# Moving tiles of four feed-forward layers, begun at four different byte offsets

## The chip, the core and the metric

The kernel runs on one core of one Trainium2 chip. The time is device microseconds of one execution of the whole program; a profile gives the span from the first to the last instruction of one such execution. One unit returns all through: the **pitch** of matmuls, which is the time from the start of one matmul to the start of the next.

## The reference

The input is 256 rows of 1024 float32 numbers. Nine stages follow one another: `ffn_a0`, `mla`, `ffn_b0`, `ffn_a1`, `nsa`, `ffn_b1`, `final` (a norm with a gain), `mix` and `peer`. The four stages named `ffn` are the feed-forward layers in question, and each of them computes

```
h = h + 0.5 * swiglu(rmsnorm(h, g), w_gate, w_up, w_down)
swiglu(x) = (silu(x @ w_gate) * (x @ w_up)) @ w_down     # 1024 -> 2816 -> 1024
```

The stages between them are attention mixers (`mla`, `nsa`, `mix`), and `peer` multiplies the rows with two tables of 16384 x 1024 numbers and combines them by gates.

## The kernel before

Every matrix product is made of three. Each float32 operand is split into a high part in the type that TensorE multiplies in one pass (`fp32r`) and the rest, the low part; high by high, high by low and low by high are summed in PSUM. `Stream` reads all weights in the order of use, in pieces of 128x1024, by SyncE's DMAs. ScalarE makes the high part (`wh`, lines 180 and 189) and VectorE the low part (`wl`, lines 204 and 209). Each half of a piece is multiplied by the norm's gain on the way where there is one.

At the end of each stage `down` adds the product to the 256 rows in `c.x` and makes the operand of the next stage. `Norm` transposes the rows by TensorE (line 331), ScalarE copies them out of PSUM into the tile `xth` (high part, line 338) and VectorE writes the rest into `xtl` (line 339). Each tile has 8 slices of 256 columns, one for each 128 of the 1024 input numbers. The rows' factors `rstd` are made beside that by `rstd_of` (ScalarE line 318, GpSimd lines 320 and 322) and are applied after the product.

In `ffn` the weights are the stationary operand, 128x128 at a time, and a slice of `xth` or `xtl` is the moving operand, 128x256 (lines 581 to 583). A chunk is 256 of the 2816 hidden numbers for gate and up. It takes 8 slices x 4 blocks x 3 products = 96 matmuls. With 11 chunks a layer has 1056 such matmuls, and the four layers have 4224. Each matmul has a weight load of its own, of 128 columns. The mixers use the same tiles the other way round: `xth` and `xtl` are stationary there and the weights move (`linear`, line 261). In `peer` weights are stationary again (line 1645), with 3072 matmuls on a slice of `xth` or `xtl` and 384 on the tiles `gb` and `qbd`.

`Lined` places tiles of 256 bytes and more on multiples of 256 bytes within a partition, `LINE`. Small tiles such as `ss`, `ms`, `rstd` and `nm`, of 32 bytes per buffer, stand behind one another in the same pool. Weight tiles begin on such a multiple, and a block of 128 weights is 512 bytes, so every weight load begins on one. The list `OFF` gives, in elements of 4 bytes, where in `xth` the slices begin, for each `Norm` that `down` makes; the first layer's comes from `take_norm`. Before, `xth` is padded by 48 elements and `xtl` by 16; `xtl` stands right behind `xth`, with no filling, that is 192 bytes past a multiple of 256, and its slices begin at `(off + 16) % 64`. Counted from a multiple of 256 bytes, the high and low slices therefore begin at the same byte: at 192 (48 elements) in the four feed-forward layers and in `peer`, and at 0 in `mla`, `nsa` and `mix`. A slice is 1024 bytes, so all eight slices of a tile have the same offset.

`flush` puts the leftovers of one chunk (its evacuation, and a matmul on line 552 that spreads the row factors) into the next chunk's first matmuls.

Of the kernel before, what the change touches and what calls it, by code (L numbers as in the profile page):

```python
# [8 lines left out]
F32R = mybir.dt.float32r  # L9
# [7 lines left out]
P = 128  # L17
D = 1024
NT = 2
KD = D // P  # L20
# [19 lines left out]
    _n += _w  # L40
NCOLS = _n + 8
LINE = 256
OFF = [0, 48, 48, 0, 48, 0, 48]


class Lined:


    def __init__(self, pool, late=False):
        self.pool, self.tags, self.late, self.over = pool, set(), late, 0  # L50

    def fill(self, name):
        if name == "xtl":
            return
        if self.over:
            self.pool.tile([P, (LINE - self.over) // 4], F32, name=name + "_fill", tag=name + "_fill", bufs=1)
        self.over = 0
# [197 lines left out]
def rounds(nc, sets, start, stop):  # L255

    for p, (a, b) in enumerate(((0, 0), (0, 1), (1, 0))):
        for out, st_, mv in sets:  # L260
            nc.tensor.matmul(out, st_[a], mv[b], start=start and p == 0, stop=stop and p == 2)  # L261
# [9 lines left out]
def ps_tile(c, tag, name):  # L271
    return c.psum.tile([P, 512], F32, name=name, tag="bank", bufs=8)


def uid(c, s):
    c.n += 1
    return f"{s}_{c.n}"


def lined(c, pool):  # L280
    return c.lines.setdefault(pool, Lined(pool, pool is c.pool))


def wt(c, shape, tag, bufs, dt=F32):
    return lined(c, c.pool).tile(shape, dt, name=uid(c, tag), tag=tag, bufs=bufs)


def st(c, shape, tag, bufs, dt=F32):
    return c.sp.tile(shape, dt, name=uid(c, tag), tag=tag, bufs=bufs)
# [23 lines left out]
def rstd_of(c, src, n):  # L313

    nc = c.nc
    junk = c.sp.tile([P, D], mybir.dt.bfloat16, name=uid(c, "junk"), tag="junk", bufs=1)
    ss = wt(c, [P, 1], "ss", 4)
    nc.scalar.activation(junk[:, :n], src, AF.Square, accum_out=ss)
    m = wt(c, [P, 1], "ms", 4)
    nc.gpsimd.tensor_scalar(m, ss, 1.0 / n, EPS, op0=ALU.mult, op1=ALU.add)  # L320
    r = wt(c, [P, 1], "rstd", 8)
    nc.gpsimd.tensor_tensor(r, m, c.mhalf, op=ALU.pow)
    return r

# [50 lines left out]
def behind(t, off):  # L375

    return t[:, off:off + KD * 256].rearrange("p (k q) -> p k q", k=KD)


class Norm:  # L380
# [2 lines left out]

    def __init__(self, c, off=0):
        self.c = c
        self.hi = behind(wt(c, [P, KD * 256 + 48], "xth", 1, F32R), off)
        self.lo = behind(wt(c, [P, KD * 256 + 16], "xtl", 1, F32R), (off + 16) % 64)
        self.rs = [None] * NT

    def turn(self, t, half):  # L390
# [2 lines left out]
    def stats(self, t):  # L393
        self.rs[t] = rstd_of(self.c, self.c.x[t], D)
# [13 lines left out]
class FinalNorm(Norm):  # L408
# [9 lines left out]
    def again(self, t):  # L418
        r_ = rstd_of(self.c, self.c.x[t], D)
        self.c.nc.gpsimd.tensor_tensor(self.rs[t], self.rs[t], r_, op=ALU.mult)  # L420
# [17 lines left out]
def take_norm(c, kind=Norm):  # L438
    n = c.norm
    c.norm = None  # L440
    if n is None:
        n = kind(c, 48)
        n.all()
    return n.hi, n.lo, n.rs

# [35 lines left out]
def down(c, hi, lo, KT, scale, nxt, rate=0):  # L481
# [26 lines left out]
    if nxt:  # L508
        n = c.norm = nxt(c, OFF[c.norms])
        c.norms += 1  # L510
# [22 lines left out]
def ffn(c, nxt):  # L533

    nc = c.nc
    with c.tc.tile_pool(name=uid(c, "ffn"), bufs=1) as pool:
        c.sp = pool = Lined(pool)
        hi, lo, rs = take_norm(c)
        ah = pool.tile([P, NFT, 256], F32R, name=uid(c, "ah"))
        al = pool.tile([P, NFT, 256], F32R, name=uid(c, "al"))  # L540
# [56 lines left out]
class Attn:  # L597
# [40 lines left out]
    def post(self, i, u, ops):  # L638
        c, nc = self.c, self.c.nc
        nh = u[2]  # L640
        s = self.rows() if self.rows else st(c, [P, 512], "s", self.ns)
        nm = wt(c, [P, 4], "nm", 4)
        ps = self.ps.pop(i)
        for h in range(nh):
            sl = slice(h * u[3], (h + 1) * u[3])
            nc.vector.tensor_tensor_reduce(s[:, sl], ps[:, sl], ops.bias(u, h), -ops.scale, -PAD, ALU.add, ALU.min,  # L646
                                           nm[:, h:h + 1])
        if self.sink is not None:
            self.e[i] = self.sink(u, nm)
        self.s[i] = s, nm  # L650
# [90 lines left out]
def mla(c, nxt):  # L741
    nc = c.nc
    scale = (MN + MR) ** -0.5
    with c.tc.tile_pool(name="mla", bufs=1) as pool:
# [5 lines left out]
        if 2:  # L750
            c.ws.segment(c.ends["mla_wo"], pool, 2, 3)
        rope, causal = (c.early[n] for n in ("rope", "causal"))
        hi, lo, rs = take_norm(c)
        cq = [T([P, MQ], f"cq{t}") for t in range(NT)]
        ckv = [T([P, MKV + MR], f"ckv{t}") for t in range(NT)]
# [22 lines left out]
        def evac_in(ci, t, ps):  # L778
            if ci == 0:
                nc.scalar.activation(cq[t], ps, AF.Copy, scale=rs[t])  # L780
                rq[t] = rstd_of(c, cq[t], MQ)
                c.pend.append(lambda: transpose_to(c, cq[t], t, cqh, cql, [0, 1, 2], "mla_q_norm"))
            else:
                nc.scalar.activation(ckv[t], ps, AF.Copy, scale=rs[t])
                rkv[t] = rstd_of(c, ckv[t][:, :MKV], MKV)
                nc.gpsimd.tensor_copy(kr[t], ckv[t][:, None, MKV:])
                rotate(kr[t], t, 1)
                c.pend.append(lambda: transpose_to(c, ckv[t], t, ckh, ckl, [0, 1], "mla_kv_norm"))
# [171 lines left out]
def nsa(c, nxt):  # L960
    nc = c.nc
    with c.tc.tile_pool(name="nsa", bufs=1) as pool:
# [15 lines left out]
        h1 = T([P, 2, GG, 16], "h1")  # L978
        h1r = T([P, GG, 4, 16], "h1r")
        hi, lo, rs = take_norm(c)  # L980
        r8, rneg = [], []

# [639 lines left out]
def peer(c, nxt):  # L1622
# [4 lines left out]
    with ExitStack() as ctx:  # L1627
# [7 lines left out]
        n = Norm(c, 48)  # L1635
# [28 lines left out]
        with c.tc.tile_pool(name="peer1", bufs=1) as pp:  # L1664
# [138 lines left out]
            n = len(work)  # L1803
# [14 lines left out]
        with c.tc.tile_pool(name="peer2", bufs=1) as pp:  # L1818
# [40 lines left out]
            def prep(n):  # L1859

                if n >= NK:
                    return
                i = V_ORDER[n]
                a = stage[i // 4][:, (i % 4) * 256:(i % 4 + 1) * 256]
                nc.vector.tensor_tensor(a, a, G[:, i], op=ALU.mult)
                if n < 2:
                    h, l = (pp.tile([P, 256], F32R, name=uid(c, t), tag=t, bufs=3) for t in ("hj", "hg"))
                else:
                    h, l = ring[0][:, n % 4, 0], ring[0][:, n % 4, 1]
                nc.scalar.activation(h, a, AF.Copy)  # L1870
                nc.vector.tensor_sub(l, a, h.bitcast(F32))  # L1871
                C[n] = h, l
                if n % 4 == 3:
                    del stage[i // 4]
                    load(n // 4 + 2)

            ring = []
            hot(0)
            b = 0
# [11 lines left out]
                    hot(b + 1)  # L1891
                    b += 1

            ring.append(wt(c, [P, 8 * 256 + 16], "xtl", 1, F32R)[:, 16:][:, :2048].rearrange("p (a b q) -> p a b q", a=4, b=2))
            acc = [[ps_tile(c, "acc", uid(c, "acc")) for _ in range(2)] for t in range(NT)]
            for n in range(NK - 2):
                w = [c.ws.next() for _ in range(2)]
                prep(n + 2)
                h, l = C.pop(n)
                a = n == 0  # L1900
                tss = [slice(t * P, (t + 1) * P) for t in range(NT)]
                rounds(nc, [(acc[t][f], (h[:, ts], l[:, ts]), w[f]) for f in range(2) for t, ts in enumerate(tss)],
                       a, False)
                if n == 8:
                    xr = wt(c, [P, NT * D + 48], "xth", 1)[:, :NT * D].rearrange("p (t d) -> p t d", t=NT)
                    for t in range(NT):
                        nc.gpsimd.dma_start(xr[:, t], xs[t])
            w = {(n, f): c.ws.next() for n in (NK - 2, NK - 1) for f in range(2)}
# [166 lines left out]
```

## Time and profile before

| what | value |
|---|---|
| median of 3 runs | 2009.03 us (2008.43 to 2010.54) |
| the profiled execution, whole time | 2011.29 us |
| its span | 2009.5 us |
| granted TensorE clock, mean over the span | 0.994 |
| TensorE matmuls, busy share | 98% |
| VectorE, busy share | 74% |

The whole time of the profiled execution is its span and 1.8 us around it. A busy TensorE is not TensorE at its peak: the record of a 128x256 matmul is 276 ns long, but the next one starts after some 113 ns. How fast TensorE gets on is read from the starts, or from the number of matmuls in a stretch without idle time.

### The profile page before, as it was taken

How to read it: one execution, taken by the hardware profiler on the slowest of the kernel's cores; microseconds unless marked ns; L12 is line 12 of the kernel's file. 1: busy time of each engine (PE TensorE's matmuls, PEld its weight loads, DVE VectorE, ACT ScalarE, POOL GpSimd, SP SyncE). 2: the span in 40 equal slices, each digit the busy share in tenths (PEclk: the TensorE clock that was granted, in tenths of full speed). 3: DMA queues.
4: the chain of work that ended last, by engine and by line, in shares of the span. 5: the costliest groups of instructions: out<-in, count | busy, mean ns of one | idle time of the engine just before them, and what ended most of it. 6: DMA issues, size and time to landing. Idle time of an engine off the chain costs nothing.

```text
span 2009.5 us, 35124 instructions
## 1 busy us (share of the span) xinstructions
PE 1978.0 (98%) x13284; PEld 1806.2 (90%) x13284; DVE 1488.9 (74%) x2747; ACT 1099.9 (55%) x1803; POOL 329.7 (16%) x398
## 2 busy tenths in 40 slices
PE   8999999999999999999999999999999999999999
PEld 8998989988998877899887789999999998888887
DVE  6765667765875788777489878999688877767675
ACT  6554756544554467665387655445444545554543
POOL 2210413202330432332044100000000000000000
PEclk9999999999999989999999999999999999999999
DMA  6665425664766322376643565776654548777774
GB/s 213 196 197 164 144 90 193 195 203 160 248 225 217 125 77 87 124 259 200 199 148 106 166 201 180 251 243 229 212 180 167 168 158 285 239 243 244 236 250 158
DMA packets 105385, 380.76 MB, mean 189 GB/s; under 512 B 12032, under 2 KB 12224, under 8 KB 104960
## 3 DMA queue, kind: packets, MB, share of 16 engines
q1 hardware_dynamic: 93600, 335.76, 51.1%
q0 software_dynamic: 11616, 42.77, 6.3%
q8 instruction: 104, 1.70, 0.4%
q14 instruction: 65, 0.53, 0.1%
HBM read 360.63 MB, written 17.85 MB: 188 GB/s over the span
## 4 chain that ended last, share of the span: by engine, by line
PE 88%; DVE 7%; ACT 2%; issue 2%; POOL 2%; DMA 0%; SPq 0%; ACTq 0%; DVEq 0%; POOLq 0%
PE acc L261 30%; PE A L1645 17%; PE gu L582 8%; PE gu L583 8%; PE gu L581 8%; PE lin L261 5%; PE G L1843 3%; PE acc L268 2%; PE q L1645 2%; DVE wl L209 2%; PE up L261 1%; PE tr L331 1%; DVE wl L204 1%; DVE s L646 1%; PE po L841 1%
## 5 line engine op out<-in xcount | busy, mean ns | idle before, releaser
L180 ACT ACTIVATE wh<-raw 128x1024 fp32r<-128x1024 f32 (+1 forms) x402 | 422.5, 1057 | 333.0 <-issue 142.2
L204 DVE TENSOR_TENSOR wl<-raw,wh 128x1024 fp32r<-128x1024 f32 (+1 forms) x402 | 486.0, 1219 | 130.0 <-PE acc L261 95.0
L209 DVE SCALAR_TENSOR_TENSOR wl<-raw,cols_sb,wh 128x512 fp32r<-128x512 f32 (+4 forms) x488 | 412.7, 896 | 70.2 <-ACT wh L189 35.2
L582 PE MATMUL gu<-xth,wl 128*128 128x256 f32 x1408 | 391.4, 278 | 1.5 <-DVE wl L209 1.5
L581 PE MATMUL gu<-xth,wh 128*128 128x256 f32 x1408 | 391.7, 278 | 0.0
L583 PE MATMUL gu<-xtl,wh 128*128 128x256 f32 x1408 | 390.6, 277 | 0.0
L189 ACT ACTIVATE wh<-raw,cols_sb 128x512 fp32r<-128x512 f32 (+4 forms) x480 | 303.1, 697 | 55.2 <-PE gu L583 35.3
L582 PEld LDWEIGHTS gu<-xth,wl 128*128 128x128 f32 x1408 | 264.9, 188 | 2.8 <-DVE wl L209 2.3
L581 PEld LDWEIGHTS gu<-xth,wh 128*128 128x128 f32 x1408 | 265.9, 189 | 0.7 <-ACT ah L567 0.4
L583 PEld LDWEIGHTS gu<-xtl,wh 128*128 128x128 f32 x1408 | 265.0, 188 | 0.0
L261 PE MATMUL acc<-wh,xtl 128*128 128x512 f32 x992 | 245.2, 389 | 0.0
L261 PEld LDWEIGHTS acc<-wh,xtl 128*128 128x128 f32 x992 | 186.2, 188 | 38.7
L1645 PE MATMUL A<-xth,wh 128*128 128x256 f32 x1024 | 205.3, 282 | 0.0
L1645 PE MATMUL A<-xtl,wh 128*128 128x256 f32 x1024 | 200.7, 277 | 0.0
L1645 PE MATMUL A<-xth,wl 128*128 128x256 f32 x1024 | 200.5, 277 | 0.0
L1645 PEld LDWEIGHTS A<-xtl,wh 128*128 128x128 f32 x1024 | 154.9, 188 | 0.0
L1645 PEld LDWEIGHTS A<-xth,wl 128*128 128x128 f32 x1024 | 154.9, 188 | 0.0
L1645 PEld LDWEIGHTS A<-xth,wh 128*128 128x128 f32 x1024 | 154.9, 189 | 0.0
L261 PE MATMUL acc<-wl,xtl 128*128 128x512 f32 x496 | 132.6, 389 | 0.0
L1659 ACT ACTIVATE x<-A 128x512 f32<-128x512 f32 x64 | 38.3, 598 | 171.6 <-PE A L1645 149.0
L1871 DVE TENSOR_TENSOR xtl<-x,xtl 128x256 fp32r<-128x256 f32 x126 | 53.6, 425 | 97.2 <-ACT xtl L1870 97.2
L261 PEld LDWEIGHTS acc<-wl,xtl 128*128 128x128 f32 x496 | 93.1, 188 | 19.3
(440 smaller groups left out, 3172.2 us busy)
## 6 DMA issues: line engine op xcount, KB each, us to landing
raw<-in_peer_u SPq DMA_DIRECT2D x128, 512.0 KB, 3.7
raw<-in_peer_v SPq DMA_DIRECT2D x128, 512.0 KB, 3.6
raw<-in_gu_a SPq DMA_DIRECT2D x88, 512.0 KB, 4.4
raw<-in_gu_b SPq DMA_DIRECT2D x88, 512.0 KB, 4.1
raw<-in_wd_a SPq DMA_DIRECT2D x44, 512.0 KB, 4.2
raw<-in_wd_b SPq DMA_DIRECT2D x44, 512.0 KB, 4.2
raw<-in_mix_in SPq DMA_DIRECT2D x34, 512.0 KB, 3.5
a_spill<-x POOLq DMA_DIRECT2D x30, 512.0 KB, 3.6
```

The lines of the kernel that those rows point to most:

```text
L180: nc.scalar.activation(h[:, :n], r[:, :n], AF.Copy)
L189: nc.scalar.activation(h[:, o:o + w], r[:, o:o + w], AF.Copy, scale=g)
L204: nc.vector.tensor_sub(l[:, :n], r[:, :n], h[:, :n].bitcast(F32))
L209: nc.vector.scalar_tensor_tensor(l[:, b], r[:, b], g, h[:, b].bitcast(F32), op0=ALU.mult, op1=ALU.subtract)
L261: nc.tensor.matmul(out, st_[a], mv[b], start=start and p == 0, stop=stop and p == 2)
L268: nc.tensor.matmul(out, st_[a], mv[b], start=False, stop=p == 2 and i == 1)
L581: nc.tensor.matmul(out, wh[:, js], hi[:, k], start=k == j % 2 == 0, stop=False)
L582: nc.tensor.matmul(out, wl[:, js], hi[:, k], start=False, stop=False)
L583: nc.tensor.matmul(out, wh[:, js], lo[:, k], start=False, stop=k == KD - 1 and j % 2 == 1)
L1645: nc.tensor.matmul(ps, w[a][:, k * P:(k + 1) * P], x[b][:, k], start=k == a == b == 0, stop=k == KD - 1 and a == 1)
L1843: nc.tensor.matmul(ps[:, (q + r_) * NK:(q + r_ + 1) * NK], hj[:, r_], hg[:, r_], start=True, stop=True)
L1871: nc.vector.tensor_sub(l, a, h.bitcast(F32))
```

## The change

The slices of the moving tiles begin at byte 208 in `ffn_a0` (52 elements), at 224 in `ffn_b0` (56), at 160 in `ffn_a1` (40) and at 176 in `ffn_b1` (44), in place of 192 in all four. High and low slices keep one offset between them. `mla`, `nsa`, `mix` and `peer` stay at 0 and 192 as they were. For that both tiles get 64 elements of padding, and `xtl` begins on a multiple of 256 bytes like other tiles. Room is made by fewer buffers for four small tiles: `ss` 2 in place of 4, `ms` 3 in place of 4, `rstd` 6 in place of 8, `nm` 3 in place of 4. The number of instructions does not change. The list `OFF` runs over `mla`, `ffn_b0`, `ffn_a1`, `nsa`, `ffn_b1`, `mix`, `peer`.

```diff
-OFF = [0, 48, 48, 0, 48, 0, 48]
+OFF = [0, 56, 40, 0, 44, 0, 48]
...
     def fill(self, name):
-        if name == "xtl":
-            return
         if self.over:
...
-    ss = wt(c, [P, 1], "ss", 4)
+    ss = wt(c, [P, 1], "ss", 2)
     nc.scalar.activation(junk[:, :n], src, AF.Square, accum_out=ss)
-    m = wt(c, [P, 1], "ms", 4)
+    m = wt(c, [P, 1], "ms", 3)
     nc.gpsimd.tensor_scalar(m, ss, 1.0 / n, EPS, op0=ALU.mult, op1=ALU.add)
-    r = wt(c, [P, 1], "rstd", 8)
+    r = wt(c, [P, 1], "rstd", 6)
...
     def __init__(self, c, off=0):
         self.c = c
-        self.hi = behind(wt(c, [P, KD * 256 + 48], "xth", 1, F32R), off)
-        self.lo = behind(wt(c, [P, KD * 256 + 16], "xtl", 1, F32R), (off + 16) % 64)
+        self.hi = behind(wt(c, [P, KD * 256 + 64], "xth", 1, F32R), off)
+        self.lo = behind(wt(c, [P, KD * 256 + 64], "xtl", 1, F32R), off)
...
     if n is None:
-        n = kind(c, 48)
+        n = kind(c, 52 if kind is Norm else 48)
         n.all()
...
-        nm = wt(c, [P, 4], "nm", 4)
+        nm = wt(c, [P, 4], "nm", 3)
...
-            ring.append(wt(c, [P, 8 * 256 + 16], "xtl", 1, F32R)[:, 16:][:, :2048].rearrange("p (a b q) -> p a b q", a=4, b=2))
+            ring.append(wt(c, [P, 8 * 256 + 64], "xtl", 1, F32R)[:, :2048].rearrange("p (a b q) -> p a b q", a=4, b=2))
...
-                    xr = wt(c, [P, NT * D + 48], "xth", 1)[:, :NT * D].rearrange("p (t d) -> p t d", t=NT)
+                    xr = wt(c, [P, NT * D + 64], "xth", 1)[:, :NT * D].rearrange("p (t d) -> p t d", t=NT)
```

## Rows read from the trace of the kernel before

**Rows 1.** The page: busy us (share of the span) x instructions, and the chain.

```profile
PE 1978.0 (98%) x13284; PEld 1806.2 (90%) x13284; DVE 1488.9 (74%) x2747; ACT 1099.9 (55%) x1803; POOL 329.7 (16%) x398
...
PE 88%; DVE 7%; ACT 2%; issue 2%; POOL 2%; DMA 0%; SPq 0%; ACTq 0%; DVEq 0%; POOLq 0%
```

**Rows 2.** Windows, all engines, of the third feed-forward layer: us busy (x instructions).

```profile
480.00:603.00 123.00, 122.64 (x1069) 122.20 (x1069) 93.18 (x113) 71.70 (x113) 45.07 (x42) 1.00 0.67 218
```

**Rows 3.** Windows, PE alone, in the layers: us, PE busy (x matmuls), granted clock.

```profile
33.00:88.00 55.00, 55.00 (x488) 1.00 0.67 210
94.00:134.00 40.00, 40.00 (x342) 1.00 0.62 191
322.00:418.00 96.00, 96.00 (x849) 1.00 0.64 200
505.00:601.00 96.00, 96.00 (x850) 1.00 0.73 237
852.00:948.00 96.00, 96.00 (x849) 1.00 0.70 230
```

**Rows 4.** The same windows view, in first chunks of layers one, three and two.

```profile
14.70:25.50 10.80, 10.80 (x94) 1.00 0.73 243
483.00:495.50 12.50, 12.50 (x108) 1.00 0.66 211
312.90:316.90 4.00, 4.00 (x36) 1.00 0.01 4
```

**Rows 5.** Timeline of PE in the first layer, round 92 us: start, us, instruction.

```profile
92.16 0.28 PE L583 MATMUL gu<-xtl,wh 128*128 128x256 f32 x1
92.36 0.60 PE L929 MATMUL rb<-t,t 32*16 32x256 f32 x2
92.89 0.39 PE L581 MATMUL gu<-xth,wh 128*128 128x256 f32 x1
```

**Rows 6.** The chain in the second chunk of the third layer: start, us, what.

```profile
501.04 1.29 DVE wl L209
502.38 0.39 PE gu L582
```

**Rows 7.** Timeline of PE in `peer`, two blocks of 24 matmuls between gates.

```profile
1454.28 0.40 PE L1645 MATMUL A<-xtl,wh 128*128 128x256 f32 x2
...
1456.63 0.40 PE L1645 MATMUL A<-xth,wl 128*128 128x256 f32 x2
1456.87 1.06 PE L1843 MATMUL G<-hg,hj 128*128 128x128 f32 x8
...
1458.23 0.39 PE L1645 MATMUL A<-xth,wl 128*128 128x256 f32 x2
...
1460.27 0.39 PE L1645 MATMUL A<-xth,wl 128*128 128x256 f32 x2
```

**Rows 8.** Timeline of PE in `mix`, weights 256 wide moving from byte 0.

```profile
1022.42 0.40 PE L261 MATMUL lin<-wl,xth 128*128 128x256 f32 x2
...
1025.06 0.40 PE L261 MATMUL lin<-wh,xth 128*128 128x256 f32 x2
```

**Rows 9.** Timeline of PE in `mla`, weights 288 wide, from bytes 0, 128, 0.

```profile
208.50 0.43 PE L261 MATMUL lin<-wh,xth 128*128 128x288 f32 x2
...
209.30 0.43 PE L261 MATMUL lin<-wh,xth 128*128 128x288 f32 x2
...
210.10 0.42 PE L261 MATMUL lin<-wh,xth 128*128 128x288 f32 x2
```

**Rows 10.** Timeline of PE in `nsa`, weights 48 wide.

```profile
696.82 0.38 PE L261 MATMUL lin<-wl,xth 128*128 128x48 f32 x2
...
701.73 0.38 PE L261 MATMUL lin<-wh,xtl 128*128 128x48 f32 x2
```

**Rows 11.** The tile `xth`: its two writers, duration ns min/median/max.

```profile
L338 ACT ACTIVATE xth<-tr x28: 575/598/600, 7.1 to 1012.9; 128x512 fp32r<-128x512 f32 x28
L339 DVE TENSOR_TENSOR xtl<-tr,xth x28: 679/691/693, 7.8 to 1013.7; 128x512 fp32r<-128x512 f32 x28
```

**Rows 12.** Source lines 320, then 646: what ended idle time before them.

```profile
  ACT junk L318: 186.5, 19
...
  PE sc L826: 11.8, 10
  PE sc L1187: 3.2, 2
  PE sc L1390: 0.4, 1
```

**Rows 13.** Lines by form: the exponentials that read `nm` (48 of 96).

```profile
L659 ACT ACTIVATE s<-s,nm 128x256 f32<-128x256 f32 x48 | 23.8, 498 | 1.9 <-DVE nm L646 1.7
```

## The prediction

> **What bounds the kernel now.** I read the page first. TensorE is busy 98% of the span and has 88% of the chain that ended last [rows 1], so what one matmul takes is what counts. I then read the windows of one feed-forward layer: in 123 us PE is busy 122.6 us, VectorE 93 us and ScalarE 72 us [rows 2]. The others have a quarter of the time in reserve there, so a slower TensorE is paid in full, and so is a slightly faster one.
>
> Third, I read windows of PE alone inside the layers and counted starts. A window counts every matmul that overlaps it, and a record lasts longer than two pitches, so two of the count are already under way when the window opens. In the third layer, 96.0 us / 848 = 113.2 ns; in the second and fourth, 96.0 / 847 = 113.3 ns; in the first, from 33 to 88 us, 55.0 / 486 = 113.2 ns. But in the same layer, from 94 to 134 us, 40.0 / 340 = 117.6 ns [rows 3]. The instruction, the shape, the addresses modulo 256 and the granted clock (1.00 in all five) are the same. So one offset, 192, has two speeds, which I call **fast** (113.3) and **slow** (117.6).
>
> What switches between them is seen at the borders. In the first layer the slow stretch begins where a foreign matmul of line 929 is put into the stream at 92.36 us [rows 5]. In the third layer a slow stretch ends after PE waited for `wl` of line 209 to end at 502.3 us [rows 6]. In `peer`, also at byte 192, a block before a group of gate matmuls runs at 2.35 us / 20 = 117.5 ns and the one behind it at 2.04 us / 18 = 113.3 ns [rows 7]. Without an interruption a speed lasts for hundreds of matmuls.
>
> Slow matmuls in the layers today: 340 after 94 us, 92 and 106 in the first chunks of layers one and three [rows 3, 4], and a stretch of 34 between two interruptions in the second layer [rows 4]. I estimate such a stretch for each of the four layers. That is about 675, and at 4.3 ns each **2.9 us** are lost to the slow speed now.
>
> **What other offsets show.** In `mix` weights 256 wide move from byte 0 past stationary blocks that also begin at 0: 2.64 us / 22 = **120.0 ns** [rows 8]. This is worse than either speed at 192. In `mla` weights 288 wide give 0.80 us / 6 = 133.3 ns from byte 0, and again 0.80 / 6 = 133.3 ns from byte 128 [rows 9]. So 128 is no better than 0 there. With 48 columns moving, the pitch is 4.91 us / 44 = **111.6 ns** [rows 10]; little streams past then, so I take this as what the weight load alone needs, and as the floor for a faster offset. No row shows 160, 176, 208 or 224.
>
> **The change part by part.**
>
> *Offsets.* Each layer has 1056 matmuls on the path. From fast to slow throughout, a layer costs 1056 x 4.3 ns = 4.5 us; from fast to 120.0, 1056 x 6.7 = 7.1 us; from fast to the floor it gains 1056 x 1.7 = 1.8 us. For all four together, with the 2.9 us that are lost already:
> - all fast: -2.9 us
> - all at the floor: -2.9 - 7.2 = -10.1 us
> - all slow: 18.2 - 2.9 = +15.3 us
> - all at 120.0: 28.3 - 2.9 = +25.4 us
>
> Between these ends I choose by distance. 224 and 160 lie 32 bytes from 192, halfway to 256 (which is 0 again) and to 128, and both of those are bad in rows 8 and 9. Midway between 113.3 and 120.0 is 116.7, and the nearest row is the slow speed. So I price the second and third layers as slow throughout: 9.1 us, less about 0.7 us that they lose already (some 170 slow matmuls), that is **+8.4 us**. 208 and 176 lie only 16 bytes off, and I leave the first and fourth layers as they are: **0**.
>
> *Writes to shifted slices.* ScalarE and VectorE write the slices in 575 to 600 and 679 to 693 ns, over offsets 0 and 192 alike [rows 11]; I take 0. If a new offset made each of the 28 writes by ScalarE a tenth longer, that would be 1.7 us in all, and only in part on the path.
>
> *Fewer `ss`, `ms`, `rstd`.* With 2 buffers the third `Square` in a row must wait until GpSimd has read the first one's sum. GpSimd stood idle for that sum 186.5 us in 19 waits [rows 12], so it takes each at once, and the norms come in pairs with most of a stage between them. Behind the `Square` on ScalarE wait the `wh` copies, which TensorE needs. I take 0.
>
> *`nm` with 3 buffers.* VectorE's write for a unit now waits for the exponential of the unit three before, not four. The plan issues that exponential one step after its own unit, so two steps before the buffer is needed. All waits before line 646 now end with a PE score [rows 12], none with ScalarE. With that cover gone, one exponential of 0.5 us [rows 13] would hold VectorE and the `wl` behind it. I take 0.
>
> Sum: +8.4 us. The profiled execution took 2011.3 us, 2.3 above the median of the runs, so it would become 2019.7 us, and the median 2009.0 + 8.4 = **2017.4 us**.
>
> **A rule against this.** The rows show one product at 113.3, 117.6 and 120.0 ns, by offset and by what came before [rows 3, 8]. The Trainium skill, page "TensorE: Matmul & The Clock Gate", section "Step-by-step: what each phase is for", says that TensorE reads the moving operand and the next weights through two independent ports, so that loading takes nothing from the running matmul. The page "SBUF — State Buffer", section "Specifications (TRN2)", gives lines of 16 bytes, and all offsets here are whole lines. By these two the offset would be worth 0 and the time would stay at 2009. This trace does not agree with the first as far as 0 and 192 go; on steps of 16 bytes no row decides.
>
> **The rivals.**
>
> *No change that can be measured.* The speed is set by the interruptions alone, these stay, and neighbours of 192 behave like it. For it: both speeds exist at one and the same offset. Against it: 120.0 at offset 0 is a third speed. Time: from all fast, -2.9, to about one layer gone slow, +4: 2006 to 2013. 0.2% is 4.0 us, about what a measurement of this kernel can tell from no change.
>
> *Faster.* The mechanism is one: the new offsets let the load run at its own 111.6 ns, whatever came before. For it: the slow speed shows that something beside the load holds TensorE up, and an offset could take that away. Against it: 1.7 ns is all that is left of the fast speed, and bad values lie on both sides. Removing only the slow stretches gives 2.9 us and is not measurable. It becomes a gain from a mean pitch under 113.0 ns on: today's mean is 113.3 + 2900 / 4224 = 114.0, and 4.0 us are 0.95 ns each. At most 1999; likely 2001 to 2005.
>
> *Much slower.* The dip at 192 is narrow and all four layers run at 117.6 to 120.0: +15 to +25 us, 2024 to 2034. For it: 0 and 128 are bad alike and 192 is the only good offset that rows show. Against it: 16 bytes are little beside the 64 that separate 192 from either.
>
> **How the numbers follow.** My case, one to three layers slow, +4 to +15 us (2013 to 2024), has 0.38; much slower 0.15; no change 0.31; faster 0.16. So slower is 0.53, same 0.31, faster 0.16. The range goes from 2004, which leaves out a little over half of the faster case (0.09), to 2028, which leaves out half of the much slower one (0.08). My case alone spans 2013 to 2024.
>
> **What would show it.** In the profile after, windows of PE alone in each layer's last nine chunks, some 96 us: about 849 matmuls is fast, 818 is slow, 802 is 120.0. I expect about 818 in the second and third layers, 849 in the fourth, and the records of slow matmuls some 5 ns longer. `peer`, `mix` and the 512-wide products should stay as they are. The prediction is wrong if 224 and 160 count 849 or more, if 208 and 176 lose too, or if a layer counts above 855. It is also wrong if ScalarE now ends waits before line 646, or GpSimd those before line 318.

## The result, and the profile after

| | before | after |
|---|---|---|
| median of the runs | 2009.4 us | 2029.7 us |
| ratio, with its 95% interval | | 1.0099 [1.0084, 1.0114] |
| the profiled execution | 2011.3 us | 2029.4 us |
| its span | 2009.5 us | 2027.6 us |

The change made the kernel slower by 1.0%, 20.3 us in the medians and 18.1 us between the two spans. In the profile after, lines stand two lower than before (581 is now 579). First, busy us by engine, from the page.

```profile
PE 1995.4 (98%) x13284; PEld 1823.0 (90%) x13284; DVE 1489.0 (73%) x2747; ACT 1101.6 (54%) x1803; POOL 330.0 (16%) x398
```

TensorE has 17.4 us more in its matmuls (PE) and 16.8 in its weight loads (PEld), and no other engine has more than 2 [rows 1]. Next, windows of PE alone in the four layers: us, busy (x matmuls), granted clock, DMA share, GB/s. Byte 208 has the first two, then come 224, 160 and 176.

```profile
35.00:90.00 55.00, 55.00 (x464) 1.00 0.63 202
97.00:137.00 40.00, 40.00 (x346) 1.00 0.62 193
328.00:424.00 96.00, 96.00 (x814) 1.00 0.60 188
516.00:612.00 96.00, 96.00 (x812) 1.00 0.70 224
868.00:964.00 96.00, 96.00 (x807) 1.00 0.65 217
```

Where 96 us held 849 matmuls [rows 3] they now hold 807 to 814. With two of each count already under way, as in the prediction, the pitches are 119.0 and later 116.3 ns at 208, 118.2 at 224, 118.5 at 160 and 119.3 at 176, at the same granted clock. Counted from the starts, as in the map below, they are 119.2 and 116.7, 118.3, 118.7 and 119.3: a window is true to some 0.4 ns. No layer has the 113.3 ns of before. Over the two stretches of the first layer the mean went from 95 us / 826 = 115.0 to 95 / 806 = 117.9 ns. So the four layers lose 2.9, 4.9, 5.3 and 6.0 ns per matmul. For the 864 matmuls of each layer's last nine chunks that makes 19.1 x 864 = 16.5 us of the 18.1; the rest, 1.5 us by the starts of matmuls, lies in the first two chunks.

The same by line, and the products that were to stay: line, engine, forms xcount | busy us, mean ns | idle before.

```profile
L580 PE MATMUL gu<-xth,wl 128*128 128x256 f32 x1408 | 397.7, 282 | 1.8 <-DVE wl L207 1.8
...
L259 PE MATMUL acc<-wh,xtl 128*128 128x512 f32 x992 | 245.2, 389 | 0.0
L1643 PE MATMUL A<-xth,wh 128*128 128x256 f32 x1024 | 205.4, 282 | 0.0
```

Each record of line 580 is 4 ns longer (278 before). The 512-wide `acc` and `peer`'s `A` stand at 245.2 and 205.4 us, against 245.2 and 205.3 on the page before. VectorE keeps its cover in the third layer, 93 busy us of 128.

```profile
488.00:616.00 128.00, 127.65 (x1070) 127.25 (x1070) 93.38 (x113) 72.15 (x113) 45.16 (x42) 1.00 0.67 213
```

The edits that I had priced at nothing show no cost. Here are the writers of the shifted slices, what ended VectorE's idle time before the line that writes `nm` (now 644), and who waited for the `Square` of line 316.

```profile
L336 ACT ACTIVATE xth<-tr x28: 574/597/602, 6.5 to 1030.9; 128x512 fp32r<-128x512 f32 x28
L337 DVE TENSOR_TENSOR xtl<-tr,xth x28: 678/691/693, 7.2 to 1031.7; 128x512 fp32r<-128x512 f32 x28
...
  PE sc L824: 11.7, 10
  PE sc L1185: 3.3, 2
  PE sc L1388: 0.4, 1
...
  POOL ms L318: 186.2, 19
```

They are the rows of before, the writers within 2 ns and the waits within 0.3 us [rows 11, 12]: still PE scores ahead of line 644, and still GpSimd waiting for the sum, not ScalarE for a free buffer.

### The profile page after: what moved, and what is told of

It is laid out like the page before. It is cut to its first block, busy times and chain, and to the rows that moved or that the text cites. A ratio compares the mean times of both kernels' runs of the same rounds, so it can differ in the third digit from the quotient of the medians.

```text
span 2027.6 us, 35124 instructions
## 1 busy us (share of the span) xinstructions
PE 1995.4 (98%) x13284; PEld 1823.0 (90%) x13284; DVE 1489.0 (73%) x2747; ACT 1101.6 (54%) x1803; POOL 330.0 (16%) x398
## 4 chain that ended last, share of the span: by engine, by line
PE 89%; DVE 6%; ACT 2%; POOL 2%; issue 1%; DMA 0%; SPq 0%; ACTq 0%; DVEq 0%; POOLq 0%
PE acc L259 29%; PE A L1643 17%; PE gu L580 8%; PE gu L581 8%; PE gu L579 8%; PE lin L259 5%; PE G L1841 3%; PE acc L266 2%; PE q L1643 2%; DVE wl L207 1%; PE up L259 1%; PE tr L329 1%; DVE wl L202 1%; DVE s L644 1%; PE po L839 0%
## 5 line engine op out<-in xcount | busy, mean ns | idle before, releaser
L580 PE MATMUL gu<-xth,wl 128*128 128x256 f32 x1408 | 397.7, 282 | 1.8 <-DVE wl L207 1.8
L579 PE MATMUL gu<-xth,wh 128*128 128x256 f32 x1408 | 397.3, 282 | 0.0
L581 PE MATMUL gu<-xtl,wh 128*128 128x256 f32 x1408 | 395.8, 281 | 0.0
L259 PE MATMUL acc<-wh,xtl 128*128 128x512 f32 x992 | 245.2, 389 | 0.0
L1643 PE MATMUL A<-xth,wh 128*128 128x256 f32 x1024 | 205.4, 282 | 0.0
L563 POOL TENSOR_TENSOR u<-u,g 128x512 f32<-128x512 f32 x40 | 66.0, 1651 | 282.3 <-DVE u L560 231.8
```

The costliest lines, as they stand in the source:

```text
L563: e.tensor_tensor(u, u, g, op=ALU.mult)
L579: nc.tensor.matmul(out, wh[:, js], hi[:, k], start=k == j % 2 == 0, stop=False)
L580: nc.tensor.matmul(out, wl[:, js], hi[:, k], start=False, stop=False)
L581: nc.tensor.matmul(out, wh[:, js], lo[:, k], start=False, stop=k == KD - 1 and j % 2 == 1)
L1643: nc.tensor.matmul(ps, w[a][:, k * P:(k + 1) * P], x[b][:, k], start=k == a == b == 0, stop=k == KD - 1 and a == 1)
```

## The experiments

All edits are to the changed kernel. Where a pitch stands without a window, it is the mean distance between starts in the last nine chunks of a layer, with the few gaps over 130 ns left out, or, where two are given, in the stretches before and behind the interruption some 60 us into those chunks. Where a kernel ran once, its one time is given.

**Offsets back, the rest kept.**

```diff
-OFF = [0, 56, 40, 0, 44, 0, 48]
+OFF = [0, 48, 48, 0, 48, 0, 48]
...
-        n = kind(c, 52 if kind is Norm else 48)
+        n = kind(c, 48 if kind is Norm else 48)
```

> The changed kernel with its room and its fewer buffers, but all four layers back at byte 192. Theory O (the offsets alone cost the time): each layer's last nine chunks have steady pitches of 113.3 or 117.6 to 117.8 ns again, and the time is 2009 us, within 0.2%. Rival R (the moved tiles or the fewer buffers cost it): the pitches stay at 116.7 to 119.3 ns and the time at 2026 to 2030 us.

Measured: ratio to the kernel before 1.0001 [0.9987, 1.0014]. Windows of PE in the layers:

```profile
33.00:88.00 55.00, 55.00 (x488) 1.00 0.67 208
94.00:133.00 39.00, 39.00 (x333) 1.00 0.61 191
322.00:418.00 96.00, 96.00 (x850) 1.00 0.63 200
```

Every stretch is back, the slow one of 39.0 / 331 = 117.8 ns after 94 us among them. So the moved tiles and the fewer buffers cost nothing that is measured (the interval leaves room for 3 us), and the offsets cost the time.

**A map of all multiples of 16 bytes.** Three kernels with four offsets each (only the list and the first layer's number differ), beside the changed kernel and the one before.

```diff
-OFF = [0, 56, 40, 0, 44, 0, 48]
+OFF = [0, 28, 36, 0, 48, 0, 48]
...
-        n = kind(c, 52 if kind is Norm else 48)
+        n = kind(c, 24 if kind is Norm else 48)
```

> The four layers at bytes 0, 64, 128 and 240. Theory A (an offset that is a whole multiple of 64 bytes has a fast state, others have not): 113.3 or 117.8 ns in the first three layers, 116 to 120 ns and no 113.3 in the fourth; some 2010 to 2018 us. Rival B (192 alone is good, since there the moving tile begins 64 bytes ahead of the weights' multiple): 119 to 120 ns at 0 and some 118 to 120 at 64, 128 and 240; some 2029 to 2034 us.

> The four layers at bytes 16, 32, 48 and 80. Theory A: no layer has a steady 113.3 ns, all lie at 116 to 120 ns; 2024 to 2034 us. Rival B says the same of these four; they are here for the map. A third theory, D (the pitch rises and falls smoothly with the distance from 192), would have 80 nearer to 117 and 16 nearer to 120.

> The four layers at bytes 96, 112, 144 and 192. Theories A and B: 116 to 120 ns in the first three layers and 113.3 or 117.8 in the fourth; some 2022 to 2026 us. A fourth theory, L (the layer decides, not the byte), would have the fourth layer at 119.3 ns as in the changed kernel, where it stood at 176.

Measured: 2025.9, 2027.3 and 2021.8 us. Pitches by byte in ns, two where both were seen as steady:

| byte | ns | byte | ns | byte | ns | byte | ns |
|---|---|---|---|---|---|---|---|
| 0 | 120.0 | 64 | 117.8 | 128 | 118.7 | 192 | 113.3, 117.8 |
| 16 | 118.7, 116.7 | 80 | 120.0 | 144 | 118.7 | 208 | 119.2, 116.7 |
| 32 | 116.7 | 96 | 120.0 | 160 | 118.7 | 224 | 118.3 |
| 48 | 118.3 | 112 | 113.3 | 176 | 119.3 | 240 | 117.1 |

Windows of bytes 0, 64 and 128 in the first kernel, of 32 and 80 in the second, and of 96, 112, 144 and 192 in the third:

```profile
40.00:136.00 96.00, 96.00 (x798) 1.00 0.58 186
330.00:426.00 96.00, 96.00 (x817) 1.00 0.60 190
518.00:614.00 96.00, 96.00 (x811) 1.00 0.69 223
...
328.00:424.00 96.00, 96.00 (x825) 1.00 0.61 191
866.00:962.00 96.00, 96.00 (x803) 1.00 0.65 215
...
40.00:136.00 96.00, 96.00 (x798) 1.00 0.58 185
326.00:422.00 96.00, 96.00 (x850) 1.00 0.63 200
514.00:610.00 96.00, 96.00 (x811) 1.00 0.69 224
862.00:958.00 96.00, 96.00 (x850) 1.00 0.70 230
```

Two offsets out of sixteen hold 850 matmuls in 96 us: 192 and, as no theory of mine had it, 112. Theory A falls: 0 and 128 have neither pitch of 192, and 64 has the slow one alone, 117.8. So do B (112 is fast) and D (80 has 120.0 and 16 has 118.7 and 116.7, the other way round than D had them). The fourth layer is fast at 192, where at 176 it was not, so L falls too.

**All four layers at 208.**

```diff
-OFF = [0, 56, 40, 0, 44, 0, 48]
+OFF = [0, 52, 52, 0, 52, 0, 48]
```

> All four layers at byte 208, where the changed kernel had only the first, at 119.2 and later 116.7 ns. Theory G (the byte decides, the layer does not): each layer settles at one of these two pitches; +14 to +25 us in the four layers, 2023 to 2034 us. Rival L (the layer decides): the second layer at 118.3, the third at 118.7 and the fourth at 119.3 ns, as in the changed kernel at their own bytes.

Measured: 2029.0 us; windows of the second and third layers:

```profile
328.00:424.00 96.00, 96.00 (x825) 1.00 0.62 193
516.00:612.00 96.00, 96.00 (x808) 1.00 0.70 223
```

The second layer settles at 96.0 / 823 = 116.6 ns and the other three at 119.2, the two values of the map. The byte gives a small set of steady pitches. Which of them a layer gets is not set by the byte, and it can change at an interruption, as at 95 us in the changed kernel.

**The weights moved in place of the moving tiles.** The weight tiles begin 32 bytes later, and with them the pools that are opened behind them, the one with `ah` and `al` (the down products' stationary tiles) among them; `xth` and `xtl` lie in an earlier pool. The layers stand at 192, 224, 144 and 112, which is 160, 192, 112 and 80 past the weights.

```diff
-        c.ws.segment(len(pieces), ctx.enter_context(tc.tile_pool(name="split", bufs=1)), 4, 2)
+        split = ctx.enter_context(tc.tile_pool(name="split", bufs=1))
+        split.tile([P, 8], F32, name="front", tag="front", bufs=1)
+        c.ws.segment(len(pieces), split, 4, 2)
...
-OFF = [0, 56, 40, 0, 44, 0, 48]
+OFF = [0, 56, 36, 0, 28, 0, 48]
...
-        n = kind(c, 52 if kind is Norm else 48)
+        n = kind(c, 48 if kind is Norm else 48)
```

> The weight tiles and the pools behind them moved up by 32 bytes; the four layers' moving tiles at 192, 224, 144 and 112, that is 160, 192, 112 and 80 past the weights, modulo 256. Theory P (the difference decides): the pitches that the map of the earlier runs gives for these differences: 118.7, then 113.3 or 117.8, then 113.3, then 120.0 ns; peer, 160 past its weights, at 118.7 in its long stretch, 1096 us and more become some 9 us longer there. Rival Q (the moving start alone): 113.3 or 117.8 at 192, 118.3 at 224, 118.7 at 144, 113.3 at 112.

Measured: 2040.5 us; windows of the layers, of `peer`, and of the down product of the second layer (512 wide) in the last row, then the 256-wide run of `mix` (start, us, instruction):

```profile
38.00:88.00 50.00, 50.00 (x428) 1.00 0.62 202
100.00:136.00 36.00, 36.00 (x306) 1.00 0.61 197
326.00:422.00 96.00, 96.00 (x849) 1.00 0.63 201
508.00:604.00 96.00, 96.00 (x850) 1.00 0.72 236
860.00:956.00 96.00, 96.00 (x803) 1.00 0.66 217
1262.00:1448.00 186.00, 186.00 (x1588) 1.00 0.71 239
...
425.00:475.00 50.00, 50.00 (x223) 1.00 0.60 198
```

```profile
1031.01 0.40 PE L259 MATMUL lin<-wh,xth 128*128 128x256 f32 x2
...
1033.81 0.40 PE L259 MATMUL lin<-wh,xth 128*128 128x256 f32 x2
```

The moving byte alone says nothing any more. 192 lost its 113.3 ns (50.0 / 426 = 117.4, later 36.0 / 304 = 118.4), 224 and 144 won it, and 112 went to 96.0 / 801 = 119.9. By the difference, all four agree with the map, except that 160 now shows a second value, 117.4, beside 118.7. `peer`, 160 past its weights, has 186.0 / 1586 = 117.3 ns as well. So Q falls and P holds in the layers. In `mix`, where the moving weights now begin 32 past the stationary tiles, the run goes at 2.80 us / 24 = 116.7 ns, which is the map's pitch for 32; at 0 it had 120.0 [rows 8]. The down products, where both sides moved by 32, kept their 226.7 ns, and `peer`'s 512-wide products, where only the weights moved, went from 226.7 to 233.3. What counts is where the moving slice begins against where the weight load begins. By the starts, the 29.2 us that this span is longer than before are 9.0 in the layers, 10.1 in `peer`'s `A` and 10.1 in its 512-wide products.

**The mixers' stationary tiles moved.** There `xth` and `xtl` are the weights that are loaded, and the streams in `c.ws` move from byte 0. Layers at 192; the mixers at 64 (below), and in the second kernel at 144 (36 in place of 16).

```diff
-OFF = [0, 56, 40, 0, 44, 0, 48]
+OFF = [16, 48, 48, 16, 48, 16, 48]
...
-        n = kind(c, 52 if kind is Norm else 48)
+        n = kind(c, 48 if kind is Norm else 48)
```

> Layers at 192 as before; the stationary tiles of mla, nsa and mix begin at byte 64 in place of 0, while the weights move from 0 as before, so that the moving start stands 192 ahead of the stationary one, modulo 256. Theory P (the difference of the two starts decides): the 256-wide run of mix goes from 120.0 ns to 113.3 or 117.8 ns. Rival Q (the moving start alone decides): it stays at 120.0 ns. Whole time 2007 to 2012 us by both; the 512-wide products at 226.7 ns are expected the same by Q and open by P.

> As the last, with the stationary tiles of mla, nsa and mix at byte 144, so that the moving start stands 112 ahead of the stationary one, modulo 256. Theory P: the 256-wide run of mix at 113.3 ns, as the layer at 112 had it. Rival Q: 120.0 ns as before. Whole time 2007 to 2012 us.

Measured: 2014.3 and 2011.3 us. Timelines of the 256-wide run in `mix` (start, us, instruction), at 64 and then at 144:

```profile
1024.02 0.39 PE L259 MATMUL lin<-wh,xtl 128*128 128x256 f32 x2
...
1026.29 0.39 PE L259 MATMUL lin<-wh,xth 128*128 128x256 f32 x2
```

```profile
1022.11 0.40 PE L259 MATMUL lin<-wh,xth 128*128 128x256 f32 x2
...
1024.91 0.39 PE L259 MATMUL lin<-wh,xth 128*128 128x256 f32 x2
```

At 64 the run goes at 2.27 us / 20 = 113.5 ns, where at 0 it had 120.0 [rows 8]. Only the loaded tile had moved. At 144, the difference of 112, it has 2.80 / 24 = 116.7, not 113.3, steady from its first matmul to its last, and the next run of 21 has 118.3. In `linear` the matmuls stand in another order than in `ffn`. The differences 0, 32 and 192 have the map's pitches in `mix` too, and 112 has not. So the difference is not the whole rule; that it is the order that spoils 112 there is likely, but no run changed the order alone. The first of the two kernels is 3.0 us above the second. Its third layer stayed at 117.8 ns throughout, the slow speed of 192, which cost 3.9 us there:

```profile
505.00:601.00 96.00, 96.00 (x817) 1.00 0.71 227
```

**High and low parts at different bytes.** By layer, high/low: 192/112, 112/192, 192/0, 0/192.

```diff
-OFF = [0, 56, 40, 0, 44, 0, 48]
+OFF = [0, (28, 48), (48, 0), 0, (0, 48), 0, 48]
...
     def __init__(self, c, off=0):
         self.c = c
+        off, low = off if isinstance(off, tuple) else (off, off)
...
-        self.lo = behind(wt(c, [P, KD * 256 + 64], "xtl", 1, F32R), off)
+        self.lo = behind(wt(c, [P, KD * 256 + 64], "xtl", 1, F32R), low)
...
-        n = kind(c, 52 if kind is Norm else 48)
+        n = kind(c, (48, 28) if kind is Norm else 48)
```

> High and low slices at different bytes, high/low: 192/112 in the first layer, 112/192 in the second, 192/0 in the third, 0/192 in the fourth. Theory S (each matmul has its own price by its own byte): the first two layers at 113.3 ns; the third at (2 x 113.3 + 120.0) / 3 = 115.6 and the fourth at (113.3 + 2 x 120.0) / 3 = 117.8 ns. Rival T (the whole stream locks as one): one of the known stream pitches, or a new one, at 116.7 to 120.0 ns in the mixed layers, and perhaps in the first two as well.

Measured: 2022.0 us; windows of the second, third and fourth layers:

```profile
326.00:422.00 96.00, 96.00 (x834) 1.00 0.62 197
512.00:608.00 96.00, 96.00 (x817) 1.00 0.70 227
862.00:958.00 96.00, 96.00 (x817) 1.00 0.66 220
```

The pitches are 117.8, 115.6, 117.8 and 117.8 ns. The first layer, 192/112, has 117.8 and the second 115.6 where S had 113.3 for both: two good bytes side by side are not good. So S falls at the first step. A matmul's price is not set by its own byte alone, and what stands beside it in the stream counts. That the stream settles as a whole (T) fits, but is not shown apart from that.

**Four and eight bytes off.** Layers at 184, 196, 200 and 108.

```diff
-OFF = [0, 56, 40, 0, 44, 0, 48]
+OFF = [0, 49, 50, 0, 27, 0, 48]
...
-        n = kind(c, 52 if kind is Norm else 48)
+        n = kind(c, 46 if kind is Norm else 48)
```

> The four layers at bytes 184, 196, 200 and 108, which lie 4 or 8 bytes off the two good ones. Theory W (what counts is the line of 16 bytes in which a slice begins, and the lines at 192 and 112): 196 and 200 like 192, at 113.3 or 117.8 ns; 184 like 176 at 119.3; 108 like 96 at 120.0 ns; some 2018 to 2024 us. Rival X (the good offsets are points, and 4 bytes leave them): all four at 116 to 121 ns, some 2024 to 2034 us.

Measured: 2035.6 us; windows of the last three layers:

```profile
332.00:428.00 96.00, 96.00 (x802) 1.00 0.59 185
522.00:618.00 96.00, 96.00 (x802) 1.00 0.70 222
874.00:970.00 96.00, 96.00 (x802) 1.00 0.66 214
```

That is 120.0 ns in all of them, and in the first layer too. X holds: 4 bytes below 112 and 4 above 192 the good pitch is gone. All four of these starts lie off a multiple of 16 bytes, so whether they are bad for that or for their distance from 192 and 112 is not told apart here.

**The down products' stationary tiles moved.** `ah` and `al` at 64, 112, 144 and 16, by layer, on top of the kernel that follows.

```diff
+DOWN = {0: 16, 2: 28, 3: 36, 5: 4}
...
-        ah = pool.tile([P, NFT, 256], F32R, name=uid(c, "ah"))
-        al = pool.tile([P, NFT, 256], F32R, name=uid(c, "al"))
+        o = DOWN[c.norms]
+        ah, al = (pool.tile([P, NFT * 256 + 64], F32R, name=uid(c, n))[:, o:o + NFT * 256].rearrange(
+            "p (k q) -> p k q", k=NFT) for n in ("ah", "al"))
```

> As the kernel with layers and peer at 112, and the stationary tiles ah and al of the layers' down products at bytes 64, 112, 144 and 16, past which weights 512 wide move from byte 0. Before, all of these started at 0 and the pitch was 226.7 ns. Theory U (only where the load is as long as the stream, as at 256 columns, does the offset count): 226.7 ns in all four; 2005 to 2010 us. Theory V (the offset moves the 512-wide products too): some of the four at 224 to 238 ns, as the 512-wide products of the mixers had 231 to 236 at 64; each ns is 0.25 us in a layer.

Measured: 2013.8 us; windows of PE in the down products, at 64, 112, 144 and 16:

```profile
138.00:188.00 50.00, 50.00 (x216) 1.00 0.57 183
423.00:473.00 50.00, 50.00 (x216) 1.00 0.57 194
608.00:658.00 50.00, 50.00 (x216) 1.00 0.59 197
956.00:1006.00 50.00, 50.00 (x223) 1.00 0.62 198
```

The pitch is 233.3 ns at the first three and 226.7 at 16, as it is at 0. V holds: the offset moves a stream of 512 columns too, by 6.6 ns, though the load, at 111.6 ns by the estimate from [rows 10], is only half as long. The mixers' own 512-wide products had gone the same way with their stationary tiles at 64, from 226.9 to 233.3 ns in the first run of `mix`. Three of the four offsets are worse than 0, and none is better.

**A version that beats both.** Layers and `peer` at 112, where the layer of the map came back to 113.3 ns after each interruption.

```diff
-OFF = [0, 56, 40, 0, 44, 0, 48]
+OFF = [0, 28, 28, 0, 28, 0, 28]
...
-        n = kind(c, 52 if kind is Norm else 48)
+        n = kind(c, 28 if kind is Norm else 48)
...
-        n = Norm(c, 48)
+        n = Norm(c, 28)
```

> All four layers and peer at byte 112. Theory G (the byte decides alone, and at 112 the stream comes back to 113.3 ns after every interruption, as it did in one layer): every layer's last nine chunks at 113.3 ns, the first layer too, which loses 1.6 us at 192 after 92 us; the long stretch of peer from 1252 to 1438 us at 113.3 ns. Then 2.0 to 3.0 us less than before in the layers, 2006 to 2008 us. Rival H (what is good depends on the order of the matmuls round it): peer, which takes high and low parts in another order, is at 117 to 120 ns in that stretch; 186 us become 193 to 197 us and the whole 2013 to 2020 us.

Measured: median 2007.7 us against 2011.3 for the kernel before beside it; ratio 0.9978 [0.9965, 0.9991]. Windows of the layers and of `peer`:

```profile
36.00:132.00 96.00, 96.00 (x845) 1.00 0.63 201
320.00:416.00 96.00, 96.00 (x850) 1.00 0.63 200
503.00:599.00 96.00, 96.00 (x850) 1.00 0.72 236
849.00:945.00 96.00, 96.00 (x849) 1.00 0.70 231
1252.00:1438.00 186.00, 186.00 (x1643) 1.00 0.71 241
```

The first layer, which at 192 fell to the slow speed after 92 us in three of the four kernels that had it there, stays fast past that point. By the starts, a layer at 112 is back at 113.3 ns 13 matmuls after an interruption at the latest, every time. G holds here and H falls for this offset: `peer` keeps 186.0 / 1641 = 113.3 ns in its other order. The gain is small, as the 2.9 us lost to the slow speed had said: 2.0 us lie in the four layers of the two profiles, and for the rest of the 3.6 no run shows a place.

## Why the prediction was wrong

**What bounds the kernel** was right. TensorE's pitch was paid in full: 16.5 us of the 18.1 are counted in the layers' last nine chunks and the rest in their first two, and nothing else grew.

**The two speeds at 192** were right, and so was it that interruptions switch them. They came back with the offset, and 208 has two speeds as well. An interruption does not always switch, though: with the first layer at 192 in the kernel with the mixers at 64, the one at 92 us left it at 113.4 ns.

**The step that failed** is "208 and 176 lie only 16 bytes off, and I leave the first and fourth layers as they are: 0". They lost 2.9 and 6.0 ns per matmul. By the starts that is 2.5 and 5.8 us of the layers, 8.3 of the 9.7 us by which the two profiles are further apart than the forecast, and 176 was the worst of the four. Under it lay the choice "by distance", that the pitch changes gradually between measured offsets. The map shows no such slope: 120.0 at 96, 113.3 at 112, 118.7 at 144, and at 4 bytes from 192 it is 120.0. An offset that no row shows could be priced only by the bounds: the 18.1 us lie between "all slow" (15.3) and "all at 120.0" (25.4).

**224 and 160** I priced by the slow row, 4.3 ns; they lost 4.9 and 5.3, which with the slow stretches that they had before is 9.8 us for 8.4. The size was near, but by luck of the row: the same distance argument gave it.

**The rival "much slower"** was right in place, price and reason: all four layers between 116 and 120 ns, "The dip at 192 is narrow", 15 to 25 us. (That there is a second dip, at 112, it did not have.) I had given it 0.15. The measured 2029.7 us lies 1.7 us above the range, which I had closed at 2028 by cutting that rival in half.

**The edits at nothing** were right: fewer buffers and moved tiles give 1.0001 [0.9987, 1.0014] with the offsets back at 192, and the writes to the shifted slices take 597 and 691 ns in place of 598 and 691.

**The rule against the change** did not hold. With the moving tile where it was and only the loaded tile moved, the same products went from 120.0 to 113.5 ns in `mix`, and from 113.3 to 119.9 in the layer at 112. The Trainium skill, page "TensorE: Matmul & The Clock Gate", section "Step-by-step: what each phase is for", has two independent read ports, so that a load takes nothing from a running matmul; these runs do not agree with that as far as the pitch goes, which depends on where the load begins. What the ports do, no run shows. Whole lines of 16 bytes were not enough for a good pitch either: 14 of 16 multiples of 16 have no 113.3 ns, while starts inside a line gave 120.0 four times out of four. The Trainium skill, page "SBUF — State Buffer", section "Specifications (TRN2)", which names such lines, says nothing that tells the 14 from the two.

**What stays open**: why the differences 192 and 112 are the good ones, why 112 is not in `mix`, and why four starts off a multiple of 16 bytes are all at 120.0. The runs show that load and stream are tied together by their starts, not where in the chip they meet.

## What to carry to other kernels

Where TensorE is at its limit and every matmul has a weight load of its own, the byte at which the moving tile begins against the stationary one is a parameter worth 6% of the pitch; measure it over a whole period (here 256 bytes in steps of 16, four offsets to a run, one to a layer; that the pitch repeats after 256 was taken, not tested), and don't interpolate. Keep high and low parts at one offset, look at the steady pitch long after the last interruption, and try each width and order of matmuls by itself: what is best at 256 columns (192, 112) costs 3% at 512. Prefer an offset that comes back to its good pitch after an interruption over one that is good until the next.

## What was not expected of the hardware

The steady pitches lie on a grid. Over the last 300 matmuls of a long stretch, 113.33, 116.67 and 120.00 ns are 34, 35 and 36 times 3.33 ns, and, over the last 240, the two values at 512 columns, 226.7 and 233.3, are 68 and 70 times. Others are means over a fixed cycle of matmuls: 117.78 is 35 1/3 times, 118.33 is 35 1/2, 118.67 is 35.6. At 118.67, in the third layer of the changed kernel, the distances repeat every five matmuls, near 122, 120, 115, 117 and 119 ns. The pitches at 240, 208 and 176 repeat every seven, eight and nine matmuls in the same way (117.1, 119.2 and 119.3 are close to 35 1/7, 35 3/4 and 35 7/9 times). In these runs a stream of hundreds of equal matmuls settles into one of a few such cycles, and mostly keeps it until something interrupts it; no run here shows what the 3.33 ns are.
